# A diffusion block's input stage: token tiles turned whole into SBUF, modulation applied there on VectorE

## The chip, the cores and the metric

The kernel runs on one NeuronCore of a Trainium2 chip. The metric is the device time of one execution in microseconds (us). A core has five engines that run their own instruction streams in order and wait for each other through semaphores: PE (TensorE: matrix products and transposes), DVE (VectorE), ACT (ScalarE), POOL (GpSimd) and SP (SyncE, which issues most DMA transfers here). SBUF is the working memory; products go to eight banks of PSUM.

## The reference

One layer of a diffusion backbone: 1024 latent tokens and 128 context tokens of width 1024. Each token is normalized, scaled and shifted by vectors that come from a conditioning vector, and projected; attention in two groups of heads follows, then a gated output projection.

```python
shift, scale, gate = modulation(c, w_mod[l], b_mod[l])      # silu(c) @ w_mod + b_mod, in three parts
h = rmsnorm(xs, norm_gain[l]) * (1.0 + scale) + shift
q_a, k_a, v_a, g_a, q_b, k_b, v_b, g_b = project(h, w_in[l], qn_a[l], kn_a[l], qn_b[l], kn_b[l])
...
xs = xs + gate * merge_out(o_a, g_a, o_b, g_b, w_out[l])
```

The context tokens use the same weights with their own conditioning vector `c_ctx`.

## The kernel before

Tokens are handled in nine tiles of 128: tile 0 holds the context tokens, tiles 1 to 8 the latent ones. The 1024 channels are handled in eight chunks of 128 (`KT`). The first stage, the only one that the change touches, makes the modulated activations in transposed form (channels on partitions, tokens along the row), each as a high part and a low part (`h_at(0, ...)` and `h_at(1, ...)`), and while it does so it already computes the first gate projection, `W_GA`, for tiles 1 to 6.

A tile is loaded (`load_x`, L369), squared and summed on ACT (L382); POOL makes the reciprocal root (L384, L386); DVE scales the tile by it (`scaled`, L376).

The modulation of a chunk j comes from 1 MB of weights (`load_wm`, L328). Eight products on PE (`modulate_rows`, L350) put it into a bank of PSUM with tag D or E; it is copied to SBUF (L353), turned by two transposes on PE (`modulate`, L359), and DVE makes of it a reduction (L361) and two columns, `a_mod` (L363) and `b_col` (L365).

`transposed(j, t0, n, cond)` (L392) then does the following for chunk j of the n tiles from t0 on: one transpose a tile on PE into a bank (L397), the scaling and shift by `a_mod` and `b_col` out of that bank on ACT (L401), a cast to the high part on DVE (L406), and the low part by a subtraction on POOL (L407).

The loop over j (L441) has ten passes, called steps here. Step 0 is the start. In step j from 1 on, PE computes the gate products of chunk j-1 for tiles 1 to 4 (`first_gates`, four channel groups 0 to 3, 128x512 each), from step 2 on those of chunk j-2 for tiles 5 and 6 (`next_gates`, 128x256, the small products); among them stand the modulation and the transposes of chunk j. Tiles 7, 8 and 0 are loaded in steps 1 to 3, scaled two steps later, and turned chunk by chunk in later steps (`second`, from step `SECOND_FROM` on). The gate products of tiles 7, 8 and 0 for all chunks follow behind the loop (L511); ACT's SiLU of the first results (`put_gates`, L289) writes tiles with the tag hf, which are three buffers shared with L401.

There is no scheduler: `in_order` (L93) ties the instructions of every engine to the order in which the program writes them. So an engine that waits holds back all that stands behind it. The transfers of SP go through one queue in the order of issue. `warm(n)` (L417) puts n products of no use on PE; `WARM` says how many stand at which place of step 0.

The functions that the diff touches stand here with the lines of the profile:

Of the kernel before, what the change touches and what calls it, by code (L numbers as in the profile page):

```python
# [18 lines left out]
P = 128  # L19
D = 1024  # L20
KT = D // P
# [32 lines left out]
TURN = 2  # L54
QUERY_AT = (0, 2, 3, 6)
PAD = 2
X_FROM = 1
SECOND_FROM = 5
WARM = (8, 4, 4, 2)
WIDE = 5  # L60
LOADLEAD = 5
OUTRATE = 2.5
PADRATE = 3
# [24 lines left out]
def place(t):  # L88

    return (t - 1) % NT  # L90
# [17 lines left out]
def hybrid_step(ctx, tc, x_prompt, x_sample, cache_k_a, cache_v_a, cache_k_b, cache_v_b,  # L108
# [33 lines left out]
    def bank(tag, name):  # L142
        return ps.tile([P, 512], F32, tag=tag, name=name, bufs=BANKS[tag])
# [5 lines left out]
    def bank_tr(name):  # L149
        turn["tr"] += 1  # L150
        return bank("DE"[turn["tr"] % 2], name)
# [159 lines left out]
    with tc.tile_pool(name="st", bufs=2, side="right") as st:  # L311
# [16 lines left out]
        def load_wm(j):  # L328
            w = st.tile([P, KT, 2, P], F32, tag="wm", name=f"wm{j}", bufs=3)
            nc.sync.dma_start(w, w_mod_ss[j])  # L330
            wm.append(w)

        load_wm(0)
        nc.scalar.activation(silc, colt[:, 0:16], AF.Silu)
        bsc1 = st.tile([P, 8], F32, name="bsc1", bufs=1)
        st.tile([P, 24], F32, name="pad4", bufs=1)
# [9 lines left out]
        def modulate_rows(j):  # L346
            pm = pmod[j] = bank_tr(f"pm{j}")
            for k in range(KT):
                a = 32 * (k % 4)
                nc.tensor.matmul(pm[a : a + 32, 0:256], sil32[:, k, :], wm[j][:, k].rearrange("p s n -> p (s n)"),  # L350
                                 start=(k < 4), stop=(k >= 4), tile_position=(0, a))
            mrows[j] = st.tile([P, 256], F32, tag="mrows", name=f"mrows{j}")
            (nc.scalar.copy if j else nc.vector.tensor_copy)(mrows[j], pm[:, 0:256])  # L353

        def modulate(j):
            pm = pmod.pop(j)[:, 256:512]
            for s in range(2):
                cs = slice(P * s, P * s + P)
                nc.tensor.transpose(pm[:, cs], mrows[j][:, cs], ident)  # L359
            m4 = st.tile([P, 2, 2], F32, tag="m4", name=f"m4_{j}")  # L360
            nc.vector.tensor_reduce(m4, pm.rearrange("p (s g c) -> p s c g", s=2, c=32)[:, :, 0:2, :], axis=AX.X,  # L361
                                    op=ALU.add)
            nc.vector.tensor_scalar(a_mod[:, j, :], m4[:, 0], bsc1[:, j : j + 1], colt[:, 16 + j : 17 + j],  # L363
                                    op0=ALU.add, op1=ALU.mult)
            nc.vector.tensor_scalar(b_col[:, j, :], m4[:, 1], colt[:, 24 + j : 25 + j], None, op0=ALU.add)  # L365

        xn = {}

        def load_x(t):  # L369
            xn[t] = st.tile([P, D], F32, name=f"xn{t}", bufs=1)  # L370
            nc.sync.dma_start(xn[t], x_tile[t])

        rx = {}

        def scaled(t, r):
            nc.vector.tensor_scalar(xn[t], xn[t], r, None, op0=ALU.mult)  # L376

        def norm(t, now_=True):
            xm = xn[t]
            sq = st.tile([P, D], BF16, tag="sq", name=f"sq{t}", bufs=1)  # L380
            ss = st.tile([P, 1], F32, tag="ss", name=f"ss{t}")
            nc.scalar.activation(sq, xm, AF.Square, accum_out=ss)  # L382
            ms = st.tile([P, 1], F32, tag="ms", name=f"msx{t}")
            nc.gpsimd.tensor_scalar(ms, ss, 1.0 / D, EPS, op0=ALU.mult, op1=ALU.add)  # L384
            r = st.tile([P, 1], F32, tag="rs", name=f"rsx{t}")
            nc.gpsimd.tensor_tensor(r, ms, mhalf[:, 0:1], op=ALU.pow)  # L386
            if now_:
                scaled(t, r)
            else:
                rx[t] = r  # L390

        def transposed(j, t0, n, cond):  # L392
            px = bank_tr(f"px{j}_{t0}")
            for i in range(n):
                if j == 0 and t0 == 1:
                    warm(WARM[3])
                nc.tensor.transpose(px[:, P * i : P * i + P], xn[t0 + i][:, P * j : P * j + P], ident)  # L397
# [3 lines left out]
            nc.scalar.activation(hf[:, :w], px[:, :w], AF.Identity,  # L401
                                 scale=a_mod[:, j, cond : cond + 1], bias=b_col[:, j, cond : cond + 1])
            step = w if third(dst) else 2 * P
            for o in range(0, w, step):
                i, to = third(slice(dst.start + o, dst.start + o + step))
                nc.vector.tensor_copy(h_at(0, i, j, to), hf[:, o : o + step])  # L406
                nc.gpsimd.tensor_tensor(h_at(1, i, j, to), hf[:, o : o + step], h_at(0, i, j, to), op=ALU.subtract)  # L407

        for t in FIRST[:4]:
            load_x(t)  # L410
# [12 lines left out]
        second = [(j, 7, 2, 0) for j in range(WIDE)] + [(j, 0, 1, 1) for j in range(KT)]  # L423

        big = [bank("AABB"[ch], f"pg0_{ch}_f") for ch in range(4)]
        small = [bank("C", f"pg0_{ch}_s") for ch in (0, 2)]

        def first_gates(ch, k, part=None):
            gate_products(big[ch], W_GA, ch, slice(0, 512), k, part=part)
# [5 lines left out]
        def more():  # L435
            ready = [x for x in second if x[0] <= j]
            if ready and j >= SECOND_FROM:
                second.remove(ready[0])
                transposed(*ready[0])

        for j in range(KT + 2):  # L441
            if j == 0:
                warm(WARM[0])
                norm(1)
                modulate_rows(0)
                warm(WARM[1])
                norm(2)
                modulate(0)
                warm(WARM[2])
                norm(3)  # L450
                norm(4)
                W_GA.split()
                norm(5)
                transposed(0, 1, 4, 0)
                norm(6)
                load_wm(3)
                continue
            big_on, small_on = j <= KT, 2 <= j
            if j < KT:
                W_GA.split()  # L460
            if big_on:
                first_gates(0, j - 1, 0)
                first_gates(1, j - 1, 0)
            if j < KT:
                modulate_rows(j)
                if j + 3 < KT:
                    load_wm(j + 3)
                if X_FROM <= j < X_FROM + 3:
                    load_x(rest[j - X_FROM])
            if big_on:  # L470
                first_gates(0, j - 1, 1)
                first_gates(1, j - 1, 1)
            if j == 1:
                transposed(0, 5, 2, 0)
            if big_on:
                first_gates(2, j - 1)
            if j < KT:
                modulate(j)
                transposed(j, 1, 4, 0)
# [843 lines left out]
```

## Time and profile before

| what | us |
|---|---|
| median of three runs | 722.23 |
| all runs | 722.23, 721.96, 723.03 |
| span of the profiled execution | 721.3 |
| first gate product starts | 17.47 |
| products of tiles 7, 8 and 0 start (end of the stage) | 72.53 |

The execution that was profiled has no time of its own beside its span, so the span is compared with the median of the runs: 0.9 us lie between them. A row of the timeline gives start, duration, engine, line, operation, output and inputs, shape, count, and in brackets the idle time ahead of it with what ended it. The end of a product is modelled, and products overlap; the cost of one is read from the distance between two starts.

### The profile page before, as it was taken

The page shows a single profiled execution, that of the slowest core. Times are in us where ns is not written, and L with a number is a line of the kernel's source. Part 1 is how long each engine was busy: PE and PEld are TensorE (multiplying, and loading weights), DVE is VectorE, ACT ScalarE, POOL GpSimd, SP SyncE. Part 2 cuts the span into 40 slices and gives each one's busy share as a digit, 9 for nine tenths or more (in the row PEclk, how much of TensorE's full clock was granted, in tenths as well). Part 3 has the DMA queues.
Part 4 walks back from the last instruction along what each step waited for, and adds up shares of the span by engine and source line. Part 5 has one row for each costly group of instructions (what it writes and reads, how often), then busy time and mean ns, then how long its engine had stood idle before and what let it go on. Part 6 is the DMA issues. An engine that isn't in the chain of part 4 may idle for free. (4 is left out here: it accounts for less than half of the span.)

```text
span 721.3 us, 10622 instructions
## 1 busy us (share of the span) xinstructions
PE 698.3 (97%) x3524; PEld 559.7 (78%) x3524; DVE 457.6 (63%) x1007; ACT 411.7 (57%) x829; POOL 335.3 (46%) x355
## 2 busy tenths in 40 slices
PE   5999999999999999999999999999999999999997
PEld 2678988877777788977788888888888888887865
DVE  3466147875675872745866677577666775775653
ACT  5355411411232451158778877877787778877770
POOL 3456013332322340236666555655575557555751
PEclk9999999999999999999999999999999999999999
DMA  8961373348435115440321222121212221212323
GB/s 344 346 219 59 121 278 86 79 94 276 121 85 142 45 60 171 139 143 23 103 67 45 73 67 88 44 81 52 87 54 59 66 87 45 81 53 87 103 65 119
DMA packets 53159, 78.56 MB, mean 109 GB/s; under 512 B 6569, under 2 KB 25449, under 8 KB 52081
## 3 DMA queue, kind: packets, MB, share of 16 engines
q1 hardware_dynamic: 44928, 65.96, 28.1%
q10 hardware_dynamic: 8176, 11.94, 6.3%
q8 instruction: 28, 0.46, 0.3%
q14 instruction: 27, 0.21, 0.1%
HBM read 58.69 MB, written 19.18 MB: 108 GB/s over the span
## 5 line engine op out<-in xcount | busy, mean ns | idle before, releaser
L1108 POOL TENSOR_TENSOR pl<-pe,ph 128x512 fp32r<-128x512 f32 x130 | 167.6, 1292 | 144.7 <-DVE nm L919 67.5
L859 DVE TENSOR_REDUCE mx<-pmx 128x1 f32<-128x384 f32 x192 | 101.4, 552 | 59.5 <-PE pmx L858 58.1
L1100 ACT ACTIVATE pe<-st 128x512 f32<-128x512 f32 x146 | 86.8, 594 | 28.0 <-PE st L1098 27.1
L1104 ACT CAST ph<-pe 128x512 fp32r<-128x512 f32 x146 | 90.6, 621 | 4.8
L1118 PE MATMUL pv<-ph,v_hi 128*128 128x512 f32 x208 | 83.2, 400 | 2.2 <-DVE spare L1142 2.2
L1121 PE MATMUL pv<-pl,v_hi 128*128 128x512 f32 x208 | 82.6, 397 | 0.0
L173 POOL TENSOR_TENSOR rs_q<-ms_q,mhalf 128x8 f32<-128x8 f32 x18 | 34.8, 1931 | 82.1 <-DVE ms_q L171 82.1
L1189 PE MATMUL po<-wo,ogh 128*128 128x512 f32 x216 | 72.5, 394 | 0.2 <-DVE yt L1196 0.2
L919 DVE CUSTOM_DVE_ANT_0 sn<-sn,mask,nsink 128x512 f32<-128x512 f32 (+1 forms) x64 | 46.3, 724 | 38.3 <-PE sn L916 36.5
L858 PE MATMUL pmx<-kha,qt 128*128 128x384 f32 x192 | 61.0, 363 | 0.4 <-ACT pen L905 0.2
L1097 PE MATMUL st<-qt,kha 128*128 128x512 f32 x144 | 58.3, 405 | 1.5 <-ACT pe L1100 0.8
L1098 PE MATMUL st<-qb,kla 68*128 68x512 f32 x144 | 57.6, 400 | 1.1 <-DVE qb L878 1.1
L1120 PE MATMUL pv<-ph,v_lo 128*64 128x512 f32 x146 | 57.9, 396 | 0.0
L1121 PEld LDWEIGHTS pv<-pl,v_hi 128*128 128x128 f32 x208 | 39.4, 189 | 16.7 <-issue 0.2
L905 ACT ACTIVATE pen<-sn,nm 128x512 f32<-128x512 f32 (+2 forms) x72 | 45.0, 626 | 6.5 <-DVE nm L919 3.1
L1093 ACT CAST ph<-st 128x512 fp32r<-128x512 f32 x62 | 36.4, 587 | 19.9 <-PE st L1092 18.7
L1118 PEld LDWEIGHTS pv<-ph,v_hi 128*128 128x128 f32 x208 | 39.4, 189 | 10.5 <-ACT ogh L1154 2.4
L1189 PEld LDWEIGHTS po<-wo,ogh 128*128 128x128 f32 x216 | 40.0, 188 | 6.8 <-DVE yt L1196 0.6
L1094 DVE TENSOR_TENSOR pl<-st,ph 128x512 fp32r<-128x512 f32 x62 | 42.5, 686 | 2.3 <-ACT ph L1093 1.5
L1189 PE MATMUL po<-wo,ogl 128*128 128x512 f32 x108 | 42.6, 394 | 0.0
L594 ACT ACTIVATE sqq<-pq 128x512 f32<-128x512 f32 x18 | 10.8, 599 | 53.3 <-DMA qd<-qo0q 14.4
L858 PEld LDWEIGHTS pmx<-kha,qt 128*128 128x128 f32 x192 | 35.5, 190 | 6.2 <-DVE mx L859 1.4
(216 smaller groups left out, 1700.2 us busy)
## 6 DMA issues: line engine op xcount, KB each, us to landing
qt<-qd SPq DMA_DIRECT2D x36, 256.0 KB, 3.1
wm<-in_w_mod_ss_dram SPq DMA_DIRECT2D x8, 1024.0 KB, 5.1
qd<-qo0q ACTq DMA_DIRECT2D x36, 128.0 KB, 2.4
qd<-qo1q ACTq DMA_DIRECT2D x36, 128.0 KB, 2.4
sgl<-gd SPq DMA_DIRECT2D x36, 128.0 KB, 2.1
out_dram<-yt SPq DMA_DIRECT2D x17, 256.0 KB, 2.1
xn<-in_x_sample_dram SPq DMA_DIRECT2D x8, 512.0 KB, 7.0
wg<-in_w_mod_g_dram SPq DMA_DIRECT2D x4, 1024.0 KB, 7.9
```

The source lines that it names most:

```text
L858: nc.tensor.matmul(pm[:, 0:384], lhs, kha[:, g, 3 * b : 3 * b + 3, :], start=True, stop=True)
L859: nc.vector.tensor_reduce(mx[:, h, b : b + 1], pm[:, 0:384], axis=AX.X, op=ALU.max)
L919: nc.vector.tensor_tensor_reduce(s, s, mask[:, m0 : m0 + n], -1.0, nsink[:, 4 * g + h : 4 * g + h + 1], op0=ALU.add, op1=ALU.min, accum_ou ...
L1097: nc.tensor.matmul(s, kh, qtile[i], start=True, stop=False)
L1098: nc.tensor.matmul(s, kl, qbtile[i], start=False, stop=True)
L1100: nc.scalar.activation(pe, s, AF.Exp)
L1104: nc.scalar.copy(ph, pe)
L1108: nc.gpsimd.tensor_tensor(pl, pe, ph, op=ALU.subtract)
L1118: nc.tensor.matmul(pv, two, ph, start=(b == 0), stop=False)
L1120: nc.tensor.matmul(pv[0:64, :], vl, ph, start=False, stop=False)
L1121: nc.tensor.matmul(pv, two, pl, start=False, stop=last)
L1189: nc.tensor.matmul(po[n], a, wo_parts[KT * n + k][lo], start=(k == KS[0] and p == 0), stop=(k == KS[-1] and p == 2))
```

## The change

A tile is turned as a whole, right behind its scaling: `turn_tile` makes the eight transposes of a tile into two banks, and copies each bank into a new SBUF tile `xT`, the first on ACT, the second on DVE (tile 4: both on ACT). `affine` replaces `transposed`: the scaling and shift of a chunk reads `xT` in SBUF, on DVE instead of ACT; the cast and the subtraction stay where they were. The scaled tiles share five buffers instead of having nine.

In step 0, the loads of tiles 1 to 4 are issued ahead of the first modulation weights, and tiles 1 to 4 are turned before the first product. Tiles 5 and 6 are scaled and turned in step 1; tiles 7, 8 and 0 in steps 2, 3 and 4. `second` holds tiles 7 and 8 and tile 0 for all chunks, from step 4 on.

```diff
-X_FROM = 1
-SECOND_FROM = 5
-WARM = (8, 4, 4, 2)
-WIDE = 5
+X_FROM = 0
+SECOND_FROM = 4
+WARM = (8, 4, 6)
...
-        load_wm(0)
...
+        xT = st.tile([P, KT, TOK], F32, name="xT", bufs=1)
+
         def load_x(t):
-            xn[t] = st.tile([P, D], F32, name=f"xn{t}", bufs=1)
+            xn[t] = st.tile([P, D], F32, tag="xn", name=f"xn{t}", bufs=5)
             nc.sync.dma_start(xn[t], x_tile[t])
 
+        for t in FIRST[:4]:
+            load_x(t)
...
-        def transposed(j, t0, n, cond):
-            px = bank_tr(f"px{j}_{t0}")
...
+        def turn_tile(t, tags):
+
+            at = slice(P * place(t), P * place(t) + P)
+            for c in range(2):
+                px = bank(tags[c], f"px{t}_{c}")
+                for i in range(4):
+                    k = 4 * c + i
+                    nc.tensor.transpose(px[:, P * i : P * i + P], xn[t][:, P * k : P * k + P], ident)
+                (nc.vector.tensor_copy if c and t != 4 else nc.scalar.copy)(
+                    xT[:, 4 * c : 4 * c + 4, at], px.rearrange("p (k n) -> p k n", n=P))
+
+        def affine(j, t0, n, cond):
+
             w = P * n
             dst = slice(P * place(t0), P * place(t0) + w)
             hf = st.tile([P, 512], F32, tag="hf", name=f"hf{j}_{t0}", bufs=3)
-            nc.scalar.activation(hf[:, :w], px[:, :w], AF.Identity,
-                                 scale=a_mod[:, j, cond : cond + 1], bias=b_col[:, j, cond : cond + 1])
...
+            nc.vector.tensor_scalar(hf[:, :w], xT[:, j, dst], a_mod[:, j, cond : cond + 1],
+                                    b_col[:, j, cond : cond + 1], op0=ALU.mult, op1=ALU.add)
+            i, to = third(dst)
+            nc.vector.tensor_copy(h_at(0, i, j, to), hf[:, :w])
+            nc.gpsimd.tensor_tensor(h_at(1, i, j, to), hf[:, :w], h_at(0, i, j, to), op=ALU.subtract)
...
+        load_wm(0)
         W_GA.load()
+        load_wm(1)
         load_x(5)
+        W_GA.load()
         load_x(6)
-        load_wm(1)
+        load_wm(2)
         W_GA.load()
-        load_wm(2)
+        load_x(7)
+        load_x(8)
...
                 warm(WARM[0])
                 norm(1)
+                norm(2)
+                turn_tile(1, "AB")
+                norm(3)
+                warm(WARM[1])
+                turn_tile(2, "AB")
+                norm(4)
+                turn_tile(3, "DE")
                 modulate_rows(0)
-                warm(WARM[1])
-                norm(2)
+                turn_tile(4, "AB")
                 modulate(0)
+                affine(0, 1, 4, 0)
...
             if j < KT:
-                transposed(j, 5, 2 if j < WIDE else 4, 0)
+                if j == 1:
+                    for t in (5, 6):
+                        scaled(t, rx.pop(t))
+                        turn_tile(t, "DE")
+                    affine(0, 5, 2, 0)
+                affine(j, 5, 2, 0)
             if X_FROM + 1 < j <= X_FROM + 4:
                 t = rest[j - X_FROM - 2]
                 scaled(t, rx.pop(t))
+                turn_tile(t, "DE")
```

Three places show how this moves the instructions. Names: `pm` is the modulation's bank, `px` a bank of transposes, `pg_3_f` the gate products of channel group 3 for tiles 1 to 4, `pg_0_s` small products, `xn` a scaled tile. In the changed kernel the lines of the same work are L357 (L359), L359 to L363 (L361 to L365), L378 (L376), L384 (L382), L401 (L397), L402 (the copies into `xT`), L410 (the scaling and shift) and L413 (L406).

PE, step 3 before, from the transposes of the modulation on:

```order
L359 MATMUL pm_456<-ident,mrows_465 128x128 x2
L397 MATMUL px_1_482<-ident,xn_178 128x128
L397 MATMUL px_1_482<-ident,xn_180 128x128
L397 MATMUL px_1_482<-ident,xn_182 128x128
L397 MATMUL px_1_482<-ident,xn_184 128x128
L262 MATMUL pg_3_f<-h_0_2_117,whiga_372 128x512
L263 MATMUL pg_3_f<-h_0_2_117,wloga_373 128x512
L258 MATMUL pg_3_f<-h_0_2_125,whiga_372 128x512
L397 MATMUL px_5_494<-ident,xn_188 128x128
L397 MATMUL px_5_494<-ident,xn_190 128x128
```

PE, step 3 of the changed kernel, from the same place:

```order
L357 MATMUL pm_523<-ident,mrows_532 128x128 x2
L261 MATMUL pg_3_f<-h_0_2_117,whiga_436 128x512
L262 MATMUL pg_3_f<-h_0_2_117,wloga_437 128x512
L257 MATMUL pg_3_f<-h_0_2_125,whiga_436 128x512
L401 MATMUL px_0_559<-ident,xn_203 128x128 x4
L401 MATMUL px_1_565<-ident,xn_203 128x128 x4
L261 MATMUL pg_0_s<-h_1_0_131,whiga_354 128x256
```

Six transposes of tiles scaled long ago have gone, and eight transposes of tile 8 (`xn_203`) stand ahead of the small products.

DVE, step 3 before; `xn_333` is tile 7, turned from step 5 on:

```order
L361 TENSOR_REDUCE m_3_478<-pm_456 128x4
L363 TENSOR_SCALAR a_mod<-m_3_478,bsc_172,colt 128x2
L365 TENSOR_SCALAR b_col<-m_3_478,colt 128x2
L406 CAST h_0_3_118<-hf_1_487 128x512
L406 CAST h_1_2_132<-hf_5_497 128x256
L376 TENSOR_SCALAR xn_333<-xn_333,rsx_432 128x1024
L235 TENSOR_TENSOR wloga_522<-rawga_376,whiga_521 128x512
```

DVE, step 3 of the changed kernel; `xn_203` is the tile that PE turns in the same step:

```order
L359 TENSOR_REDUCE m_3_543<-pm_523 128x4
L361 TENSOR_SCALAR a_mod<-m_3_543,bsc_170,colt 128x2
L363 TENSOR_SCALAR b_col<-m_3_543,colt 128x2
L410 TENSOR_SCALAR hf_1_547<-xT,a_mod,b_col 128x512
L413 CAST h_0_3_118<-hf_1_547 128x512
L410 TENSOR_SCALAR hf_5_554<-xT,a_mod,b_col 128x256
L413 CAST h_1_2_132<-hf_5_554 128x256
L378 TENSOR_SCALAR xn_203<-xn_203,rsx_499 128x1024
L402 COPY xT<-px_1_565 128x4x128
```

Two scalings and a copy have come to DVE; the scaling of the tile stands behind both pairs of scaling and cast.

ACT, start of the kernel before: the squares of tiles 1 to 4, the high part of the weights, the square of tile 5:

```order
L382 ACTIVATE sq_212,ss_213<-xn_178 128x1024
L382 ACTIVATE sq_235,ss_236<-xn_180 128x1024
L382 ACTIVATE sq_253,ss_254<-xn_182 128x1024
L382 ACTIVATE sq_261,ss_262<-xn_184 128x1024
L233 CAST whiga_269<-rawga_186 128x512
L382 ACTIVATE sq_275,ss_276<-xn_188 128x1024
```

ACT, start of the changed kernel:

```order
L384 ACTIVATE sq_215,ss_216<-xn_177 128x1024
L384 ACTIVATE sq_223,ss_224<-xn_179 128x1024
L402 COPY xT<-px_0_231 128x4x128
L384 ACTIVATE sq_243,ss_244<-xn_181 128x1024
L402 COPY xT<-px_0_255 128x4x128
L384 ACTIVATE sq_267,ss_268<-xn_183 128x1024
L402 COPY xT<-px_0_275 128x4x128
L402 COPY xT<-px_0_298 128x4x128
L402 COPY xT<-px_1_304 128x4x128
L232 CAST whiga_320<-rawga_187 128x512
```

Copies of turned tiles now stand between the squares: the square of tile 3 behind the copy of tile 1, that of tile 4 behind the copy of tile 2.

More of the change, by code (lines that the diff above doesn't have):

```diff
@@ L390, in norm @@
                 rx[t] = r
-        def transposed(j, t0, n, cond):
-            px = bank_tr(f"px{j}_{t0}")
[L394 to L397, printed above, removed]
+        def turn_tile(t, tags):
[8 more added lines that the diff above has]
+        def affine(j, t0, n, cond):
             w = P * n
@@ L400, in transposed @@
             hf = st.tile([P, 512], F32, tag="hf", name=f"hf{j}_{t0}", bufs=3)
-            nc.scalar.activation(hf[:, :w], px[:, :w], AF.Identity,
-                                 scale=a_mod[:, j, cond : cond + 1], bias=b_col[:, j, cond : cond + 1])
[L403 to L410, printed above, removed]
+            nc.vector.tensor_scalar(hf[:, :w], xT[:, j, dst], a_mod[:, j, cond : cond + 1],
[4 more added lines that the diff above has]
+        load_wm(0)
         W_GA.load()
+        load_wm(1)
         load_x(5)
+        W_GA.load()
         load_x(6)
-        load_wm(1)
+        load_wm(2)
         W_GA.load()
-        load_wm(2)
+        load_x(7)
+        load_x(8)
+        small = [bank("C", f"pg0_{ch}_s") for ch in (0, 2)]
         def warm(n):
@@ L422, in hybrid_step @@
         rest = [7, 8, 0]
-        second = [(j, 7, 2, 0) for j in range(WIDE)] + [(j, 0, 1, 1) for j in range(KT)]
-        big = [bank("AABB"[ch], f"pg0_{ch}_f") for ch in range(4)]
-        small = [bank("C", f"pg0_{ch}_s") for ch in (0, 2)]
+        second = [x for j in range(KT) for x in ((j, 7, 2, 0), (j, 0, 1, 1))]
         def first_gates(ch, k, part=None):
@@ L438, in more @@
                 second.remove(ready[0])
-                transposed(*ready[0])
+                affine(*ready[0])
         for j in range(KT + 2):
@@ L444, in hybrid_step @@
                 norm(1)
+                norm(2)
[5 more added lines that the diff above has]
+                turn_tile(3, "DE")
                 modulate_rows(0)
-                warm(WARM[1])
-                norm(2)
+                turn_tile(4, "AB")
                 modulate(0)
-                warm(WARM[2])
[L450 to L456, printed above, removed]
+                affine(0, 1, 4, 0)
+                W_GA.split()
+                load_wm(3)
+                load_x(0)
+                big = [bank("AABB"[ch], f"pg0_{ch}_f") for ch in range(4)]
+                norm(5, False)
+                norm(6, False)
+                warm(WARM[2])
                 continue
@@ L467, in hybrid_step @@
                     load_wm(j + 3)
-                if X_FROM <= j < X_FROM + 3:
-                    load_x(rest[j - X_FROM])
             if big_on:
@@ L472, in hybrid_step @@
                 first_gates(1, j - 1, 1)
-            if j == 1:
-                transposed(0, 5, 2, 0)
             if big_on:
@@ L478, in hybrid_step @@
                 modulate(j)
-                transposed(j, 1, 4, 0)
+                affine(j, 1, 4, 0)
             if big_on:
```

## The prediction

> **What bounds the kernel now.** I read the page first (busy time by engine), then the windows of the first 75 us, the only stretch that the change edits, then the timeline of each engine in them.
>
> ```profile
> span 721.3 us, 10622 instructions
> PE 698.3 (97%) x3524; PEld 559.7 (78%) x3524; DVE 457.6 (63%) x1007; ACT 411.7 (57%) x829; POOL 335.3 (46%) x355
> ...
> 5.00:10.00 5.00, 4.76 (x25) 1.37 (x23) 0.00 (x0) 1.85 (x3) 0.68 (x2) 1.00 1.01 415
> 15.00:20.00 5.00, 2.86 (x21) 1.31 (x21) 2.24 (x5) 2.43 (x4) 3.25 (x5) 0.89 0.99 413
> 35.00:40.00 5.00, 5.00 (x44) 3.80 (x42) 3.54 (x7) 2.78 (x5) 2.47 (x2) 1.00 0.88 351
> ```
>
> In a window's row stand its length, the busy time of PE, PEld, DVE, ACT and POOL, then the granted clock, the DMA share and GB/s. PE is busy for 97% of the span, and for all of a window such as 35 to 40 us. So a microsecond taken from PE's work after the start, or added to its waiting, moves the end by about as much. Before 17 us PE mostly waits for data, and DMA is full (415 GB/s). One step of the loop over j (step 3) shows what PE does there:
>
> ```profile
> 34.98 0.38 PE L359 MATMUL pm<-ident,mrows 128*128 128x128 f32 x2
> 35.20 0.60 PE L397 MATMUL px<-ident,xn 128*128 128x128 f32 x4
> 35.55 0.47 PE L262 MATMUL pg_f<-h,whiga 128*128 128x512 f32 x1
> 35.87 0.39 PE L263 MATMUL pg_f<-h,wloga 128*128 128x512 f32 x1
> 36.10 0.40 PE L258 MATMUL pg_f<-h,whiga 128*128 128x512 f32 x1
> 36.34 0.38 PE L397 MATMUL px<-ident,xn 128*128 128x128 f32 x2
> ```
>
> Four transposes hold PE from 35.20 to 35.55, and the product behind them takes 0.32 instead of 0.23 us to its successor: 0.44 us, or **0.11 us for a transpose**. The three products of channel 3 behind them take 0.79 us.
>
> **Term 1, transposes (-3.1 us).** Both kernels have 72. Before, 4 stand ahead of the first product and 68 behind it. Now the 32 of tiles 1 to 4 stand ahead of it, and 40 behind. 28 x 0.11 = 3.1 us leave the stretch in which PE is full.
>
> **Term 2, the steps that turn tiles 7, 8 and 0 (+9.9 us).** Here the change adds a wait. In steps 2 to 4 the eight transposes follow channel 3 directly, and they need the tile scaled; the scaling stands on DVE behind this step's reduction, a_mod, b_col, and now two scalings that ACT did before and two casts. DVE's and POOL's rows of step 3 before, with an undisturbed scaling and the groups of the casts and of POOL's subtractions:
>
> ```profile
> 35.47 0.17 DVE L361 TENSOR_REDUCE m<-pm 128x4 f32<-128x16 f32 x1 [1.59 <-PE pm L359]
> 35.87 0.22 DVE L365 TENSOR_SCALAR b_col<-m,colt 128x2 f32<-128x2 f32 x1
> 37.69 1.79 DVE L376 TENSOR_SCALAR xn<-xn,rsx 128x1024 f32<-128x1024 f32 x1
> ...
> 37.53 2.54 POOL L407 TENSOR_TENSOR h<-hf,h 128x512 fp32r<-128x512 f32 x2 [2.97 <-DVE h L406]
> ...
> 10.12 0.75 DVE L376 TENSOR_SCALAR xn<-xn,rsx 128x1024 f32<-128x1024 f32 x1 [6.35 <-POOL rsx L386]
> ...
> L407 POOL TENSOR_TENSOR h<-hf,h 128x256 fp32r<-128x256 f32 x16 | 14.2, 906 | 4.3 <-DVE h L406 4.3
> L407 POOL TENSOR_TENSOR h<-hf,h 128x512 fp32r<-128x512 f32 x8 | 10.6, 1328 | 17.8 <-DVE h L406 17.8
> L406 DVE CAST h<-hf 128x256 fp32r<-128x256 f32 x16 | 9.8, 646 | 2.8 <-ACT hf L401 2.7
> L406 DVE CAST h<-hf 128x512 fp32r<-128x512 f32 x8 | 3.4, 427 | 6.7 <-ACT hf L401 6.7
> ```
>
> From L359's start (34.98) to b_col's end (36.09) are 1.1 us. The new scalings of 512 and 256 columns on DVE have no row. [...] Undisturbed, the queue is 0.43 + 0.43 + 0.22 + 0.22 + 0.75 = 2.05 us; if all but the first two ran beside POOL, 0.43 + 0.43 + 0.65 + 0.65 + 1.79 = 3.95. Between: POOL starts when the cast of 512 ends and works some 2.2 us (1.33 + 0.91), in which DVE goes at 0.75/1.79 = 0.42 of its pace. So 0.86 us for the first two; then 1.2 us of work, of which 0.9 is done in POOL's 2.2 us and 0.3 after it: 3.3 to 3.4 in all. The tile is ready 4.3 to 4.5 us after L359's start; PE arrives after 0.2 + 0.8 = 1.0. I take a wait of 3.3 us in each of three steps, between 2.1 and 4.0. Behind the waiting transposes stand the small products and the whole next step; nothing on PE overtakes them.
>
> **Term 3, step 1 (+2.5 us).** Tiles 5 and 6 are scaled and turned there one after the other. Tile 5: 1.1 + 0.43 + 0.43 + 0.75 = 2.7 us behind L359's start, against 1.0 for PE: 1.7 (2.7 if beside POOL). Tile 6's scaling stands behind DVE's copy of tile 5's second half, which waits for PE: copy 0.69 and scaling 0.75, some 1.5 us. From these 3.2 go the waits before in the same place, 0.27 and 0.42 us:
>
> ```profile
> 23.31 0.66 PE L397 MATMUL px<-ident,xn 128*128 128x128 f32 x4 [0.27 <-DVE m L361]
> ...
> 25.30 0.50 PE L262 MATMUL pg_f<-h,whiga 128*128 128x512 f32 x1 [0.42 <-DVE h L406]
> ...
> L1093 ACT CAST ph<-st 128x512 fp32r<-128x512 f32 x62 | 36.4, 587 | 19.9 <-PE st L1092 18.7
> L1094 DVE TENSOR_TENSOR pl<-st,ph 128x512 fp32r<-128x512 f32 x62 | 42.5, 686 | 2.3 <-ACT ph L1093 1.5
> ```
>
> **Term 4, the first product (+2.7 us).**
>
> ```profile
> 8.00 1.06 ACT L382 ACTIVATE sq<-xn 128x1024 bf16<-128x1024 f32 x1 [4.51 <-DMA xn<-in_x_sample_dram]
> ...
> 6.86 1.94 PE L350 MATMUL pm<-wm,sil 128*32 128x256 f32 x16
> 17.47 0.50 PE L262 MATMUL pg_f<-h,whiga 128*128 128x512 f32 x1 [1.80 <-DVE h L406]
> ...
> L386 POOL TENSOR_TENSOR rsx<-msx,mhalf 128x1 f32<-128x1 f32 x9 | 5.3, 589 | 0.8
> L384 POOL TENSOR_SCALAR msx<-ss 128x1 f32<-128x1 f32 x9 | 4.1, 455 | 7.6 <-ACT sq L382 7.2
> ```
>
> The first modulation weights (1024 KB, 2.5 us at 415 GB/s) now stand behind four tiles, so tile 1 lands at 5.5 instead of 8.0, tile 4 at 9.3 and the weights at 11.8. But the squares no longer run back to back: ACT takes the square of tile 3 behind the copy of tile 1's first half, and that of tile 4 behind tile 2's. Tile 1: 5.5 + square 1.2 (1.06 and the read of its sum, an estimate) + POOL 1.05 + scaling 0.75 = 8.5; transposes to 9.4; ACT's copy to 9.7. Tile 2 turns behind four warm-up products, about 10.4 to 11.3, its copy ends at 11.5; tile 4's square 12.7, POOL 13.8, scaling 14.5. Behind it on DVE stands the copy of tile 3's second half (0.69, to 15.2), which frees the PSUM bank that the modulation products write. So these start at **15.2, not when their weights land**. From there: products 1.1 to 1.9, eight transposes 0.9, L359 to b_col 1.1, scaling and cast 0.86: 19.2 at full clock, 20.2 at half, against 17.47. I take the latter, for the reason in term 6. If ACT and DVE kept up, weights at 11.8 would give 16; that end is kept for the range.
>
> **Term 5, the end of the stage (+1.2 us).** PE waits for ACT's first SiLU there:
>
> ```profile
> 61.46 0.38 PE L359 MATMUL pm<-ident,mrows 128*128 128x128 f32 x2
> ...
> 71.32 0.28 PE L258 MATMUL pg_s<-h,whiga 128*128 128x256 f32 x1
> ...
> 71.89 0.60 ACT L289 ACTIVATE sg<-pg_f 128x512 f32<-128x512 f32 x1
> 72.53 0.44 PE L262 MATMUL pg<-h,whiga 128*128 128x384 f32 x1 [0.94 <-ACT sg L289]
> ...
> L407 POOL TENSOR_TENSOR h<-hf,h 128x128 fp32r<-128x128 f32 x8 | 3.6, 464 | 1.7 <-DVE h L406 1.7
> ```
>
> ACT is free now, but the SiLU writes a tile that POOL must have left: behind the last L359 POOL has 1.33 + 0.91 + four pairs of 0.91 and 0.46 us, 7.7 us that begin 2.0 us after it; with the SiLU's 0.6 that is 10.3. PE takes 10.0 us for this now, and without its 18 transposes there 8.0: a wait of 2.1 or a little more in place of 0.94. Bounds: the wait gone (-0.9), or +1.6.
>
> **Term 6, the clock (+4.3 us).** Windows of PE alone (length, busy, count, clock):
>
> ```profile
> 8.71:12.12 3.41, 1.91 (x13) 1.00 1.04 419
> 15.54:18.95 3.41, 1.61 (x13) 1.00 1.02 423
> 18.95:22.36 3.41, 3.41 (x22) 0.50 1.02 423
> 233.99:237.40 3.41, 2.10 (x10) 1.00 0.65 210
> 315.91:319.32 3.41, 2.12 (x9) 1.00 0.74 173
> 319.32:322.73 3.41, 3.31 (x8) 0.50 0.93 302
> ```
>
> The clock is cut to half for exactly one stretch of 3.41 us, on a fixed grid, behind a stretch in which PE was idle for about half; 1.91 and 2.10 us busy passed, 1.61 and 2.12 did not, so the edge lies near 50 to 60% busy and is not sharp. A wait of 3.3 us cannot avoid it: split over two stretches of the grid, one holds 1.65 or more and has at most 1.76 busy. The same holds for step 1's two waits and for the start (from 12.1 to 15.5 PE has about 1.3 us of work). A cut costs half of 3.41 = 1.7 us of PE work, less where it falls on waiting; I take 1.5 for each of steps 1 to 4, and take off the 1.7 that the cut at 18.95 costs now: 6.0 - 1.7.
>
> [...]
>
> **Sum.** -3.1 + 9.9 + 2.5 + 2.7 + 1.2 + 4.3 = 17.5 us. Span 721.3 + 17.5 = 738.8; the median of the runs (722.23) lies 0.9 above the profiled span, so **739.7 us**.
>
> **Rivals.**
> - A: the waits come, but the clock is cut hardly more than now. Term 6 goes and term 4 is 1.7; taking -1.7 for today's cut gone, -3.1 + 9.9 + 2.5 + 1.7 + 1.2 - 1.7 = 10.5: 732.7; with waits of 2.1 instead of 3.3, 729. For it: the edge is blurred. Against: both rows near half.
> [...]
> - C, the other side: the scaled tile is there when PE arrives, so terms 2 and 3 vanish (before's waits of 0.7 go too), and with them the cuts: -3.1 - 0.7 + 1.7 + 1.2 - 1.7 = -2.6: 719.6. It decides itself at DVE's queue: under about 1 us from L359 to the scaled tile. b_col alone ends after 1.1, so only a scaling earlier in DVE's order would do it.
> - D: terms cancel within 1.5 us, for instance if later waits of PE took up the shift. After 80 us PE waits little, which speaks against it.
>
> **How the numbers follow.** Forecast (735 to 744) 0.60, A 0.20, B 0.11, C 0.05, D 0.04. The range 730 to 746 takes in A from waits of about 2.4 us upward and B's lower half; it leaves out C, D and what lies above 746. A measurement of this kernel tells about 0.2% (1.4 us) from no change: faster 0.05, same 0.03, slower 0.92.
>
> **What would show it.** Right: in the new profile PE idles 2 to 4 us ahead of L401 in each of steps 2 to 4, released by DVE's scaling, and about 1.5 us twice in step 1; clock rows of 0.50 follow these steps; the first product starts at 19 to 20 us; the stage ends 15 us or more later, and the rest keeps its length. Wrong: no idle time at L401 (C), clock 1.00 through steps 1 to 5 (A), or the shift shrinking after 80 us (D).

## The result, and the profile after

| what | before | after |
|---|---|---|
| median, us | 722.63 (4 runs, 721.96 to 723.38) | 749.33 (4 runs, 748.05 to 750.61) |
| span of the profiled execution | 721.3 | 746.1 (its time: 748.05) |
| first gate product starts | 17.47 | 20.70 |
| products of tiles 7, 8 and 0 start | 72.53 | 94.77 |

The changed kernel is slower: ratio 1.0369, 95% interval 1.0352 to 1.0387. The forecast was 739.7 us, range 730 to 746: the direction came as forecast, the time lies above the range. The first lines of the page after:

```profile
span 746.1 us, 10625 instructions
PE 705.4 (95%) x3518; PEld 566.4 (76%) x3518; DVE 473.9 (64%) x1047; ACT 399.6 (54%) x810; POOL 335.8 (45%) x355
```

PE's rows that carry a wait, from the timeline of the kernel after, in the stretch that the change edits:

```profile
20.70 0.47 PE L261 MATMUL pg_f<-h,whiga 128*128 128x512 f32 x1 [0.63 <-DVE h L413]
...
27.33 1.06 PE L401 MATMUL px<-ident,xn 128*128 128x128 f32 x8 [1.89 <-DVE xn L378]
29.93 1.94 PE L401 MATMUL px<-ident,xn 128*128 128x128 f32 x8 [1.53 <-DVE xn L378]
...
39.94 1.97 PE L401 MATMUL px<-ident,xn 128*128 128x128 f32 x8 [3.46 <-DVE xn L378]
...
51.93 1.07 PE L401 MATMUL px<-ident,xn 128*128 128x128 f32 x8 [3.90 <-DVE xn L378]
...
63.55 1.97 PE L401 MATMUL px<-ident,xn 128*128 128x128 f32 x8 [3.39 <-DVE xn L378]
...
86.19 0.72 PE L257 MATMUL pg_f<-h,whiga 128*128 128x512 f32 x2 [0.26 <-POOL h L414]
...
94.77 0.69 PE L261 MATMUL pg<-h,whiga 128*128 128x384 f32 x1 [3.60 <-ACT sg L288]
```

L401 holds the transposes of `turn_tile`, L378 the scaling. PE waits for the scaling in each of steps 1 to 4, 3.42 us in step 1 and 10.75 in steps 2 to 4, and at the end of the stage for the first SiLU. What stands ahead of the scaling in step 3, from the timelines of DVE and POOL:

```profile
47.86 0.17 DVE L359 TENSOR_REDUCE m<-pm 128x4 f32<-128x16 f32 x1 [3.90 <-PE pm L357]
...
48.53 0.55 DVE L410 TENSOR_SCALAR hf<-xT,a_mod,b_col 128x512 f32<-128x512 f32 x1
49.11 0.43 DVE L413 CAST h<-hf 128x512 fp32r<-128x512 f32 x1
49.45 0.41 DVE L410 TENSOR_SCALAR hf<-xT,a_mod,b_col 128x256 f32<-128x256 f32 x1
49.89 1.23 DVE L413 CAST h<-hf 128x256 fp32r<-128x256 f32 x1
51.05 0.74 DVE L378 TENSOR_SCALAR xn<-xn,rsx 128x1024 f32<-128x1024 f32 x1
...
49.61 1.36 POOL L414 TENSOR_TENSOR h<-hf,h 128x512 fp32r<-128x512 f32 x1 [5.97 <-DVE h L413]
51.20 1.17 POOL L414 TENSOR_TENSOR h<-hf,h 128x256 fp32r<-128x256 f32 x1 [0.23 <-DVE h L413]
```

DVE had been idle for 3.90 us ahead of the reduction; then six instructions pass before the scaling (a_mod and b_col, not shown, are two of them), one of them, the cast of 256 columns, stretched to 1.23 us beside POOL's subtraction; the same cast took 0.29 us at 32.95, with POOL idle. The windows of PE alone (length, busy, count, granted clock, then DMA share and GB/s) show what the waits did to the clock; 1.00 is PE's full clock, 0.50 half of it:

```profile
25.82:29.23 3.41, 1.06 (x8) 1.00 1.01 408
29.23:32.65 3.42, 2.73 (x11) 0.50 0.41 175
...
49.71:53.13 3.42, 1.20 (x11) 1.00 0.06 24
53.13:56.54 3.41, 3.41 (x15) 0.50 0.06 10
...
90.67:94.09 3.42, 0.50 (x5) 1.00 0.00 0
94.09:97.50 3.41, 2.73 (x9) 0.50 0.35 136
97.50:100.91 3.41, 3.41 (x12) 0.50 0.45 174
```

The same happens at 39.47 and 63.37 us (2.95 and 3.23 us busy at half). So there are four cuts in the steps, and two more stretches at half behind the wait for the SiLU. That last wait comes from a chain of DVE and POOL:

```profile
91.67 0.40 DVE L410 TENSOR_SCALAR hf<-xT,a_mod,b_col 128x256 f32<-128x256 f32 x1
92.10 0.43 DVE L413 CAST h<-hf 128x256 fp32r<-128x256 f32 x1
92.45 0.33 DVE L410 TENSOR_SCALAR hf<-xT,a_mod,b_col 128x128 f32<-128x128 f32 x1
92.82 0.63 DVE L413 CAST h<-hf 128x128 fp32r<-128x128 f32 x1
...
92.61 0.76 POOL L414 TENSOR_TENSOR h<-hf,h 128x256 fp32r<-128x256 f32 x1 [0.23 <-DVE h L413]
93.53 0.56 POOL L414 TENSOR_TENSOR h<-hf,h 128x128 fp32r<-128x128 f32 x1 [0.16 <-DVE h L413]
...
94.12 0.60 ACT L288 ACTIVATE sg<-pg_f 128x512 f32<-128x512 f32 x1 [12.58 <-POOL h L414]
```

A pair (tiles 7 and 8, tile 0) takes 1.7 us, from 91.67 to the next pair's start at 93.37. DVE has no gap in it, POOL waits twice.

**Where the 24.8 us of the two spans lie.** A product of 384 columns starts 0.32 us after the one before it at half clock (95.26 to 95.58) and 0.17 at full (101.33 to 101.50), so a busy microsecond at half clock loses 0.47.

| term | forecast | measured | from |
|---|---|---|---|
| 1, fewer transposes | -3.1 | about -1.4 | the stage's length less waits and cuts, see the sixth experiment |
| 2, steps 2 to 4 | +9.9 | +10.75 | 3.46 + 3.90 + 3.39 |
| 3, step 1 | +2.5 | +2.7 | 1.89 + 1.53 - 0.27 - 0.42 |
| 4, first product | +2.7 | +3.2 | 20.70 - 17.47 |
| 5, end of the stage | +1.2 | +2.9 | 3.60 + 0.26 - 0.94 |
| 6, the clock | +4.3 | +7.1 | 0.47 x (12.3 busy in four cuts + 6.1 in the last two) - 1.6 for before's cut at 18.95 |
| sum | 17.5 | 25.2 | spans: 24.8 |

The medians lie 26.7 us apart, 1.9 more than the spans. 1.3 of them come from the changed kernel, whose profiled execution was the fastest of its four: their granted clocks were 0.986, 0.980, 0.979 and 0.986, and the two lower ones belong to the times 749.63 and 750.61. So other executions of the same kernel had more stretches at half clock than the one in the table. The rest lies in the reference point, see below.

### The profile page after: what moved, and what is told of

Its sections match the earlier page's. It is cut to its first block, busy times and chain, and to the rows that moved or that the text cites. A ratio compares the mean times of both kernels' runs of the same rounds, so it can differ in the third digit from the quotient of the medians.

```text
span 746.1 us, 10625 instructions
## 1 busy us (share of the span) xinstructions
PE 705.4 (95%) x3518; PEld 566.4 (76%) x3518; DVE 473.9 (64%) x1047; ACT 399.6 (54%) x810; POOL 335.8 (45%) x355
## 5 line engine op out<-in xcount | busy, mean ns | idle before, releaser
L414 POOL TENSOR_TENSOR h<-hf,h 128x256 fp32r<-128x256 f32 (+2 forms) x32 | 30.9, 967 | 40.6 <-DVE h L413 40.6
```

## The experiments

Theory Q: the waits come from the place of the scaling in DVE's queue, behind this step's modulation. Rival W: DVE's amount of work, with the modulation on it, bounds the steps. Theory K: a wait of this length also cuts the clock, so each costs more than itself. The first five kernels are the changed kernel with one edit each, the last five join edits. Each ratio stands against runs of the kernel before on the same chip; the medians of before there were 723.53 (e1 to e4), 723.24 (e5 to e8) and 722.91 (e9, e10). Differences in us to the changed kernel, whose own before had 722.63, can be off by as much as these medians differ, up to 0.9.

**1. The scaling earlier (e1).**

```diff
+            if j == 1:
+                scaled(5, rx.pop(5))
+                scaled(6, rx.pop(6))
+            if X_FROM + 1 < j <= X_FROM + 4:
+                t = rest[j - X_FROM - 2]
+                scaled(t, rx.pop(t))
             if j < KT:
                 modulate(j)
...
                     for t in (5, 6):
-                        scaled(t, rx.pop(t))
                         turn_tile(t, "DE")
...
-                t = rest[j - X_FROM - 2]
-                scaled(t, rx.pop(t))
                 turn_tile(t, "DE")
```

> Edit: in steps 1 to 4 the scaling of the tile that is turned there stands ahead of the step's reduction on VectorE instead of behind its two modulations and two casts; nothing else moves. Theory Q (the waits come from the scaling's place in VectorE's queue): rsx of tiles 8 and 0 are ready at 43.7 and 55.1 us, 4 us before the reduction, so the tile is scaled when PE arrives. The waits of 10.75 us in steps 2 to 4 and 3.42 us in step 1 fall to under 2 us in sum, and the clock stays at 1.00 through those steps (another 5 us): about 749.3 - 17 = 732. The first product stays at 20.7, and the wait of 3.6 us for the first SiLU stays or grows. Rival W (VectorE's amount of work bounds the steps, so the wait only moves to another place of PE): the waits stay at 8 us or more in sum, time 742 or more.

Measured: 730.04 us (729.6 to 730.18), ratio 1.0081 (1.0057 to 1.0105); 19.3 us less than the changed kernel. PE's waits, as the view of waits sums them, and the one left in the steps from the timeline:

```profile
PE pg L261 <- ACT sg L288: 3.6, 1, 3.6
...
PE px L401 <- DVE xn L378: 2.2, 2, 1.2
...
33.77 1.09 PE L401 MATMUL px<-ident,xn 128*128 128x128 f32 x8 [1.19 <-DVE xn L378]
```

The 2.2 us hold 1.0 at the start; 1.2 is left in step 2, where tile 7's factor comes late. No stretch of the steps runs at half clock. Theory Q holds: five scalings stand earlier, no work is less, and nearly three quarters of the loss are gone.

**2. The waits filled (e2).**

```diff
                 px = bank(tags[c], f"px{t}_{c}")
+                for _ in range(fill if c == 0 else 0):
+                    nc.tensor.matmul(px, ident_b, ident_b.unsqueeze(1).to_broadcast([P, 4, P]), start=True, stop=True)
```

> Edit: PE does matrix products whose result nothing reads (bf16, 512 columns, some 0.24 us each: 7 and 5 in step 1, 13 in each of steps 2 to 4) into the PSUM bank of the turn just ahead of its transposes, so in the time in which it waits for the scaling. Nothing waits less. Theory K (the clock is cut because PE idles for about half of a stretch of 3.41 us): the four cuts in steps 1 to 4 go, the wait for the first SiLU and the two cuts behind it stay: 5 us less, about 744. [...]

Measured: 740.95 us (739.48 to 742.2), ratio 1.0226 (1.0196 to 1.0257), 8.4 less than the changed kernel; between the two profiled spans (746.1 and 740.2) 5.9. The stretches that hold the four turns:

```profile
26.09:29.50 3.41, 2.90 (x17) 1.00 1.03 423
...
36.33:39.74 3.41, 2.76 (x18) 1.00 0.68 284
46.57:49.98 3.41, 2.61 (x16) 1.00 0.39 154
56.81:60.22 3.41, 2.84 (x18) 1.00 0.40 154
```

The clock stays at full through all four steps, and the two cuts behind the SiLU stay. Theory K holds: products that compute nothing make the kernel faster. That the gain is larger than the 5 forecast may come in part, as an estimate, from where the stretches of 3.41 us fall: in e3, whose steps 1 to 4 are those of the changed kernel, the waits of step 1 cost two stretches (27.48 to 34.31 us at half), and the granted clocks of the changed kernel's runs go down to 0.979, where those of e2 lie between 0.995 and 0.997.

**3. Own buffers for the SiLU (e3).**

```diff
-        sg_tile.append(lambda n: st.tile([P, 512], F32, tag="hf", name=n, bufs=3))
+        sg_tile.append(lambda n: st.tile([P, D], F32, tag="xn", name=n, bufs=5)[:, 0:512])
```

> Edit: the SiLU's output at the end of the stage goes to buffers of the tiles' tag (free by then) instead of the three buffers that the modulated tiles use, so it need not wait until GpSimd has read those. Theory S (that wait is one for a buffer): the SiLU runs when channel 0 is done, before 91 us; PE's wait of 3.60 us goes, but the products of k = 7 then need GpSimd's last subtraction (about 95 us): 0 to 1.5 us of waiting is left, and without the two cuts 2 to 3.4 us more come back. Time 743 (741 to 745). Rival: PE would wait as long for the last h; time 747 or more.

Measured: 744.29 us (741.11 to 744.84), ratio 1.027 (1.0238 to 1.0302), 5.0 less. ACT's first SiLU and PE's first product of the next group:

```profile
85.08 0.60 ACT L288 ACTIVATE sg<-pg_f 128x512 f32<-128x512 f32 x1 [5.19 <-PE pg_f L257]
...
89.37 0.34 PE L261 MATMUL pg<-h,whiga 128*128 128x384 f32 x1
```

The SiLU now waits for PE, not for POOL, PE goes on without a gap, and no stretch behind it is at half. Theory S holds; 0.4 us of waiting for the last h are left.

**4. The modulation on ACT (e4).**

```diff
-            nc.vector.tensor_scalar(hf[:, :w], xT[:, j, dst], a_mod[:, j, cond : cond + 1],
-                                    b_col[:, j, cond : cond + 1], op0=ALU.mult, op1=ALU.add)
+            nc.scalar.activation(hf[:, :w], xT[:, j, dst], AF.Identity,
+                                 scale=a_mod[:, j, cond : cond + 1], bias=b_col[:, j, cond : cond + 1])
```

> Edit: the modulation of every chunk is done by ScalarE (as before the change, but out of xT) instead of VectorE; casts, subtractions and scalings stay. Theory Q (the scaling's place in the queue): only 0.4 us of VectorE's queue ahead of the scaling goes, since the modulation of 512 columns still stands ahead of its cast; each of the three waits falls from 3.4 to about 3.0 us, the cuts stay. At the end of the stage VectorE has 1.1 us for a pair (casts of 256 and 128) instead of 1.7 and GpSimd's 1.4 us is the bound, as forecast: the wait for the SiLU falls from 3.6 to about 1 us, and at least one of the two cuts behind it goes. Sum 749.3 - 1.2 - 2.6 - 1.7 = 744 (741 to 747). Rival W (the modulation on VectorE is what costs): the waits of steps 2 to 4 fall under 1 us each: 735 or less.

Measured: 745.25 us (744.38 to 746.97), ratio 1.0295 (1.0267 to 1.0324).

```profile
40.13 1.96 PE L401 MATMUL px<-ident,xn 128*128 128x128 f32 x8 [3.48 <-DVE xn L378]
52.03 1.94 PE L401 MATMUL px<-ident,xn 128*128 128x128 f32 x8 [3.58 <-DVE xn L378]
64.61 1.97 PE L401 MATMUL px<-ident,xn 128*128 128x128 f32 x8 [3.49 <-DVE xn L378]
...
94.03 0.44 PE L261 MATMUL pg<-h,whiga 128*128 128x384 f32 x1 [1.56 <-ACT sg L288]
```

The waits of the steps stay at 3.5 us, not even the 0.4 us forecast less. DVE's scaling in step 3 of this kernel shows why:

```profile
50.13 1.75 DVE L378 TENSOR_SCALAR xn<-xn,rsx 128x1024 f32<-128x1024 f32 x1
```

It starts 0.9 us earlier than in the kernel after (51.05), but now POOL's subtraction of 512 columns has begun 0.2 us ahead of it (49.93), and it takes 1.75 us instead of 0.74. In the kernel after it began ahead of POOL's next subtraction, and there the subtraction was the longer one, 1.17 us. Rival W falls for the steps. At the end of the stage it is right: the wait falls from 3.60 to 1.56, and no stretch is cut behind it. There, the modulation on DVE is what costs.

**5. The start (e5).**

```diff
+                modulate_rows(0)
                 norm(4)
+                modulate(0)
                 turn_tile(3, "DE")
-                modulate_rows(0)
                 turn_tile(4, "AB")
-                modulate(0)
```

> Edit: only the start. The first chunk's modulation products and their transposes stand on PE ahead of the turns of tiles 3 and 4, and on VectorE their reads ahead of the copy of tile 3's second half. Theory P (these products wait for the PSUM bank that this copy frees, at 16.4 us, and not for their weights): they start when the weights land, near 12 to 13 us; then tile 4 is last: scaled near 15.8, its first half copied near 16.8 to 17.1, modulated and cast by 18.0: first product at 18.1 instead of 20.7, time 749.3 - 2.6 = 746.7. Rival (the weights, or the start of the transfers as a whole, set it): first product at 20 or later, 749.

Measured: 746.63 us (745.53 to 748.98), ratio 1.0325 (1.0299 to 1.0351), 2.7 less.

```profile
11.87 1.07 PE L348 MATMUL pm<-wm,sil 128*32 128x256 f32 x16 [0.66 <-DMA wm<-in_w_mod_ss_dram]
...
17.19 0.47 PE L261 MATMUL pg_f<-h,whiga 128*128 128x512 f32 x1
```

The modulation products now wait for their weights, which land at 11.9 us, and no longer until 16.45 as in the kernel after. The weights were not what they waited for; theory P holds. Of the 3.5 us between 20.70 and 17.19, about 1.5 are not the edit's: PE ran at full pace from 7.5 us on in this execution, and e3, with the start of the changed kernel and full pace from 7.0, has its first product at 19.19. That leaves some 2.0 us for the edit.

**6 to 8. Edits together (e6: 1 and 3; e7: 1, 3 and 5; e8: 1, 3, 5 and 4).**

> Edit: the early scaling (730.0 alone) and the SiLU's own buffers (5.0 less alone) together. If the waits in the steps and the wait at the stage's end are separate costs, they add up: 730.0 - 5.0 = 725 (723.5 to 726.5), with no idle time of PE over 1.3 us after the first product and clock 1.00 from there to 110 us. If they share a cause (VectorE's amount of work, that now has to fit in less time), PE waits for h of the last k instead: 727 or more.

> Edit: early scaling, the SiLU's own buffers, and the modulation products ahead of the turns of tiles 3 and 4. By theory P 2.6 less than with the first two: 722.4, the time of the kernel before within its measurement. What then still speaks for before (no scaling wait in step 2, one pair of modulations less on VectorE) is about what 28 transposes fewer save (3.1). By its rival (the start is set by the transfers): 725.

> Edit: as the one before, and the modulation on ScalarE. Theory: with the scaling early and the SiLU's own buffers VectorE's work sets no wait of PE over 0.5 us, so this changes little: 0 to 1 us less (the waits of 0.3 and 0.4 us for h at the stage's end), or up to 1 us more (the first product waits for ScalarE, 0.9 us more, as it did with the modulation on ScalarE alone): 721.5 to 723.5. Rival (VectorE's load is still what costs): 719 or less.

Measured: e6 724.48 (722.24 to 725.97), ratio 1.0009 (0.9995 to 1.0022); e7 723.52 (721.07 to 724.73), ratio 1.0000 (0.9985 to 1.0014); e8 724.02 (722.33 to 726.64), ratio 1.0012 (0.9996 to 1.0028). So 1 and 3 add up as forecast, and with 5 the kernel is where before is. The start's edit brought 1.0 us here where 2.6 were forecast, and the intervals of e6 and e7 overlap. The modulation on ACT gives nothing more; e8 missed its range a little. Its profiled execution, the slowest of the ten, has a wait that e7 does not have: ACT's SiLU now stands behind ACT's own modulations:

```profile
74.27 0.44 PE L261 MATMUL pg<-h,whiga 128*128 128x384 f32 x1 [1.42 <-ACT sg L288]
```

e6 also measures term 1, since no stretch of its stage is cut. From its first product (18.59) to the end of the stage it takes 52.19 us, 1.69 of them waits:

```profile
70.78 0.34 PE L261 MATMUL pg<-h,whiga 128*128 128x384 f32 x1
```

That leaves 50.5 us of PE's work; before has 55.06 - 1.63 - 1.6 for its cut = 51.8. So PE's work in the stage fell by about 1.3 us with 28 transposes fewer, not by 3.1. In the changed kernel the same sum, 74.07 - 18.03 - 5.8, gives 50.2.

**9 and 10. The warm-up, and tile 7 (e9: e7 with 10 warm-up products; e10: e9 with tile 7 turned later).**

```diff
-WARM = (8, 4, 6)
+WARM = (10, 4, 6)
...
+            if j == 2:
+                turn_tile(7, "DE")
```

The second edit, of e10 alone, stands behind the loop over the small products; the turn ahead of that loop is left out in step 2.

> Edit: as the third of the last four (early scaling, own buffers for the SiLU, modulation products ahead of two turns), with 10 warm-up products at the start instead of 8. Theory H (PE starts at half pace, and the clock goes to full behind the first stretch of 3.41 us in which PE is busy for some 2.8 us or more; 8 warm-up products end near 6.95 us and leave a gap of 1 us, so it depends on where the grid of stretches falls in an execution whether that is 6 to 8.7 us or 11.3 to 12.4): with PE busy from 3.4 to 7.9 us, the clock is full by 9.5 us wherever the grid falls, the first product stands at 17 to 17.5 us in every execution, and the median falls by about half of 1.5 us: 722.8 (722.0 to 723.5). Rival (the late rise has another cause): a rise after 11 us is still seen, or the times keep their median of 723.5 and their spread.

> Edit: as the one before, and the turn of tile 7 stands on PE behind the small products of step 2 instead of ahead of them (12 products, 1.4 us). Theory Q: the last wait for a scaling (1.2 us in step 2, since tile 7's factor comes only at 36 us) then lies beside these products and goes: 1.2 us less than the one before, 721.6, which would be under the kernel before by 0.2 to 0.3%. Rival: the wait only moves to the start of step 3 (the turn's copies delay what follows): no difference.

Measured: e9 721.41 (720.82 to 724.37, 12 runs), ratio 0.9984 (0.9970 to 0.9997); e10 721.71 (720.61 to 724.16, 12 runs), ratio 0.9985 (0.9971 to 1.0000). The start of e9:

```profile
3.37 3.97 PE L431 MATMUL pg_s<-ident_b 128*128 128x512 bf16 x10 [3.37 <-DVE ident_b L314]
8.01 1.09 PE L401 MATMUL px<-ident,xn 128*128 128x128 f32 x8 [0.67 <-DVE xn L378]
...
17.34 0.47 PE L261 MATMUL pg_f<-h,whiga 128*128 128x512 f32 x1
```

PE ran at full pace from 6.7 us on here. That does not test theory H: in this execution the stretch from 3.30 to 6.72 us was full (3.35 us busy) with the first eight products already. The time went from 0.28 us above before's median of the same chip (e7) to 1.50 below, 1.8 us where theory H gave 0.7, but the intervals of the two ratios overlap, so the gain is not shown, and 2 of the 12 executions still took 724 us. In e10 the wait of step 2 went, and its rival came true: from the first product to the end of the stage it takes 52.4 us, e9 52.7, and PE waits behind it instead:

```profile
32.74 0.50 PE L261 MATMUL pg_f<-h,whiga 128*128 128x512 f32 x1 [0.46 <-DVE h L413]
...
41.01 1.07 PE L348 MATMUL pm<-wm,sil 128*32 128x256 f32 x16 [0.28 <-DVE xT L402]
```

e9 and e10 are thus the fastest of the kernels here and cannot be told apart; e9 lies 0.16% under before, with an interval that just leaves out no change.

## Why the prediction was right in direction and short in size

The median lies 9.6 us above the forecast: some 7.3 us between the two spans, 1.0 in the reference point, and 1.3 because the profiled execution of the changed kernel was its fastest. The step that failed is the end of the stage, where two terms had one fault: the chain behind the first SiLU was priced with POOL as its bound (term 5, 1.7 us short), and no cut of the clock was priced behind that wait (2.9 us of term 6). Term 1, a saving 1.7 us smaller than forecast, is the other large miss.

**Term 2 and term 3 held, in part by luck.** The waits were 3.58 us a step on the mean where 3.3 were forecast, 3.42 in step 1 where 3.2 were. e1 showed that the place in the queue is the cause, e4 that taking the two modulations off DVE gives nothing. From the first modulation to the end of the scaling, DVE took 3.26 us in each of steps 2 to 4, against 3.3 to 3.4, but two errors cancel in this. The two modulations cost more, 0.55 and 0.41 us against the cast's 0.43 (half of it for 256 columns); that was the nearest row, but not the same operation: no run before the change shows the 0.43 and 0.22 us that the sum uses for them. And beside POOL only the cast was stretched; the forecast also had the scaling slowed there, which took its undisturbed 0.74 us. What is over 3.3 in the mean comes from step 3, where the reduction began 0.91 us behind the start of L357 (46.95), not 0.48 as in steps 2 and 4; why is open.

**Term 4 came out near its number by luck.** The forecast gave 19.2 us at full clock, 20.2 with a cut at 15.5 (its parts, with the products alone at half pace, add up to 20.0). No cut came there; the products of L348 took 1.07 us. PE's work ran at half pace earlier, where the forecast had PE mostly waiting for data, although its own row of the kernel before, at 5 to 10 us, has PE busy for 4.76 us: the turn of tile 1 and the warm-up behind it, in the kernel after and then in e3, whose start is the same:

```profile
7.95 1.97 PE L401 MATMUL px<-ident,xn 128*128 128x128 f32 x8 [1.01 <-DVE xn L378]
9.71 1.91 PE L431 MATMUL pg_s<-ident_b 128*128 128x512 bf16 x4
```

```profile
8.48 1.09 PE L401 MATMUL px<-ident,xn 128*128 128x128 f32 x8 [1.48 <-DVE xn L378]
9.42 1.03 PE L431 MATMUL pg_s<-ident_b 128*128 128x512 bf16 x4
```

e3's first product stands at 19.19, the forecast at full clock. The bank that the modulation products wait for was named rightly (e5).

**Term 5 was mis-sized, +2.9 in place of +1.2.** The step that failed is "behind the last L359 POOL has 1.33 + 0.91 + four pairs of 0.91 and 0.46 us": it took POOL for the bound, at 1.37 us a pair. With the modulation moved, DVE is the bound, at 1.7 us a pair, and POOL waits for it. From the start of the last L357 (82.24) to the product (94.77) it took 12.5 us where 10.3 were forecast, and the four pairs make some 1.4 of the difference. e4 takes that load away and the wait falls by 2.0; e3 takes away the shared buffer and it goes.

**Term 6 was mis-sized, +7.1 in place of +4.3.** "A cut costs half of 3.41 = 1.7 us of PE work, less where it falls on waiting; I take 1.5 for each of steps 1 to 4" fits what the four cost (5.8 against 6.0; filling the waits gave 5.9 between the profiled spans). What is missing is the wait at the end of the stage: it was forecast at 2.1 us or more, which leaves 1.3 of a stretch busy, and no cut was priced behind it. It came with two stretches at half, 2.9 us. Rival A falls by the rows of 0.50, and e2 shows that they come from the waits. Rival B, two cuts for each wait and 746 us, rested on nothing that the trace of the kernel before shows. Its count came true at places: two stretches at half lie behind the wait for the SiLU, and neither holds a transpose. The transposes behind a wait do fill a stretch here: in the one at 39.47 us, 1.97 of the 2.95 us busy are transposes, and the clock was full behind it.

**Term 1 was mis-sized, about -1.4 in place of -3.1.** The transposes themselves got cheaper as forecast: from start to start, with what the product behind them loses, some 7.5 us for 68 before and 4.7 for 40 in e6. The products around them took more, each by an amount too small for the profile to name a cause. What it is stays open.

**The reference point was off by about 1 us.** That "the median of the runs (722.23) lies 0.9 above the profiled span" set a span of one execution against a median of others. Later executions of the kernel before list both: 721.86 for a span of 719.8, 723.27 for 721.2. A time lies some 2 us above its own span; the execution that was profiled before thus took about 723.3, above its median.

## What to carry to other kernels

When an engine's new work is made to depend on another engine's queue, place what releases it by when its inputs are ready, not by where the code reads best: DVE was idle for 3.9 us just ahead of the queue that PE then waited for. Price every wait of the bounding engine with what the clock does behind it, at the last wait as well as at the first: the last one here, of 3.60 us, lost 2.9 more to the clock. And when an engine takes over work, ask again which engine is the bound in each later chain; durations of the old bound no longer give its length (1.37 us a pair forecast by POOL, 1.7 measured on DVE).

## What the runs showed of the hardware

Laid out in stretches of 3.41 us, the first 110 us of these twelve traces show the granted clock at 1.00 or at 0.50 for a whole stretch. Apart from the stretch that holds the first warm-up product (at 3.3 to 3.4 us), the stretches at full clock behind which it was cut had PE busy for at most 1.62 us (1.06, 1.20 and 0.50 in the rows above, 1.62 at 15.52 in the kernel before), and none with 1.64 or more was followed by a cut. Three with less were not followed by one either: 1.53 us at 12.17 in the kernel after, 1.45 at 12.43 in e2 and 1.62 at 6.04 in e4; why is open. Of the stretches at half clock, the seven with at most 2.69 us busy were followed by another at half, and all with 2.87 or more by one at full. Between the two, 2.73 us at 94.09 in the kernel after and 2.81 at 76.10 in e1 were followed by one at half, 2.73 at 29.23 in the kernel after and 2.79 at 51.37 in e3 by one at full. The cut at 319 us that the prediction quotes stands behind 2.12 us busy, more than any of those in the first 110 us.

At the start, PE ran at half pace, which the length of its rows shows (1.97 and 1.09 us for the same eight transposes above; in e3 eight products of the warm-up in 3.60 us from 3.41, four in 1.03 from 9.42), although the clock column reads 1.00 there. The pace rose at 12.17 us in the kernel after and at 7.00 in e3, with the same program up to there. In e3 the warm-up filled the stretch from 3.59 to 7.00 (3.41 us busy); in the kernel after the stretches fall elsewhere, the one from 5.34 to 8.75 had 2.40, and the one behind it, with 3.42, was the first full one. In e1 2.52 us (from 4.42 on) left the pace at half, in e5 2.91 (from 4.10 on) were followed by full pace.

Where DVE and POOL ran beside each other, the one that began second was stretched in the rows above: DVE's cast of 256 columns (1.23 us at 49.89 behind POOL's start at 49.61; 0.29 at 32.95 with POOL idle), its scaling in e4 (1.75 at 50.13 behind POOL's 49.93; 0.74 where it began first, at 51.05). The pair of 1.7 us that bounds the end of the stage contains such casts, 0.63 us for 128 columns at 92.82 behind POOL's 92.61.
